# First stage of a two-block network on one core: x loaded in rows and turned on the chip, its splits in written order, angles behind them, the recurrence's constants in a feed forward

## The chip, the cores and the metric

The kernel runs on one core of a Trainium2 chip. The metric is the device time of one execution in microseconds (us), as the median of several runs. Of the engines, TensorE (PE) multiplies and transposes, VectorE (DVE) and ScalarE (ACT) work elementwise, GpSimd (POOL) does a few small operations, and SyncE (SP) issues the transfers.

## The reference, cut to what matters

x has 256 tokens of width 1024. The whole network is two blocks of four sublayers; the first block begins with the even mixer, and the change lies there and in one corner of the sublayer behind it and of the odd mixer.

```python
def even_mixer(xn, positions, w_in, w_out, ...):          # xn = rms_norm(x, norm_mix_pre[0])
    z = (xn @ w_in)                                       # 1024 -> 2048: q, k, v, u of 512 each
    q, k = partial_rope(q, positions) * HEAD_DIM**-0.5, partial_rope(k, positions)
    att = dilated_attention(q, k, v)
    ssm = s5_mixer(u, a_re, a_im, log_dt, ...)            # a_bar = exp(A * dt): sin and cos of angles
    return concatenate([att, ssm]) @ w_out

def rglru_mixer(...):                                     # in the odd mixer, after the first feed forward
    log_a = -RG_C * gate_r * softplus(-lam)               # softplus(-lam): constants of 1024 channels
    ...
x = x + rms_norm(mix, norm_mix_post)                      # then swiglu, the odd mixer, swiglu, and block two
```

## The kernel before, in words

The 256 tokens are two halves of 128 rows. A product in float32 is made of three in a faster format: each operand is split into a high half and a low half, and TensorE adds high times high, high times low and low times high. The weights stand in one array in the order in which they are used, and SP loads them (`raw_weights`, L277) into four buffers `wr` of 128x1024. ScalarE copies the high half `wh`, VectorE subtracts and writes the low half `wl` (`weights`), and six buffers hold such halves; a `wr` buffer is free when its `wl` is made. Names such as `wl_538` carry the number of a tile; `pm` are sums in PSUM, `pt` transposes in PSUM, `s`, `b`, `c` and `j` buffers in SBUF, `cpk` the packed constants.

A list scheduler orders each engine by priorities and by its own estimate of when operands are ready; the transfers on SP stay in program order unless something lets them move. Each engine then works in that order and waits wherever an operand is missing.

The stage begins in `even_mixer`. `first_linear` (L1123) makes u, the last 512 columns, from `xT`, an input that holds x already turned (channels in rows): for k = 0 and 1 a product in full float32, for k = 2 to 7 the split one. Two transposes of u on VectorE (L1172), the angles (`pos` L1162, `sincos` L575) and the setup of the recurrence's matrices of s5 (`s5_setup`) follow. The projections to k (512 to 1024), q (0 to 512) and v (1024 to 1536) take x's rows for the squares (loaded at L1165; ScalarE squares `x` into `j`) and the turned and split x for the products; k and q are turned by an angle (rope: four products and two sums of 128x64 on VectorE per half) and transposed by TensorE (L227). Then come the attention over memory, the dilated attention and the s5 states.

Some work is issued through lists with due times (`later`, `need`): s5's pieces, and `memory_whole`, which loads `memT` (L813), scales it by 16 operations of ScalarE and splits it. The small constants of the odd mixer's recurrence are written in `odd_mixer` (L1302), but depend on `cpk` alone.

Of the kernel before, what the change touches and what calls it, by code (L numbers as in the profile page):

```python
# [17 lines left out]
P = 128  # L18
# [123 lines left out]
class Net:  # L142
# [222 lines left out]
    def spread_rows(self, r):  # L365

        out, d = self.slot(), self.slot()
        for h in HALVES:
            self.ts(d[:, h * P : (h + 1) * P], self.ident, r[h], ALU.mult)
# [205 lines left out]
    def sincos(self, ang, sin, cos, tmp):  # L575
# [5 lines left out]
        self.act(sin, ang, AF.Sin)  # L581
        self.stt(tmp, ang, -1.0, ang, ALU.mult, ALU.max)
        self.ts(tmp, tmp, -1.0, ALU.mult, 0.5 * math.pi, ALU.add)
        self.act(cos, tmp, AF.Sin)
# [218 lines left out]
    def remember(self):  # L803

        self.mem_x = self.first_operand("memT", "mem_norm", TUNE["mem"])
# [24 lines left out]
    def s5_exps(self):  # L830
# [13 lines left out]
        self.act(self.lru_e, self.lru_e, AF.Exp, scale=-1.0)  # L844

    def s5_setup(self):
# [152 lines left out]
        nc.gpsimd.memset(self.TO, 0.0)  # L999
# [123 lines left out]
    def first_linear(self, gain, mat, c0, c1, whole):  # L1123
# [3 lines left out]
        k = 0  # L1127
        while k < KD:
            n = 1 if k < whole else min(2, KD - k)
            t = self.slot()  # L1130
            self.nc.sync.dma_start(out=t[:, : n * 256], in_=self.ins["xT"][:, k * 256 : (k + n) * 256])
            for i in range(n):
                (hi, lo), a = X.both(k), t[:, i * 256 : (i + 1) * 256]
                if k < whole:
                    ((raw, _, _),) = self.raw_weights([(mat, k * P, c0, c1)])
                    b = t[:, 256:512]
                    self.ts(b, a, g[k], ALU.mult)
                    for h in HALVES:
                        self.mmul(ps[h], b[:, h * P : (h + 1) * P], raw[:, : c1 - c0], k == 0, False)
                    self.act(hi, b)  # L1140
                    self.sub(lo, b, hi.bitcast(F32))
                else:
                    (ws,) = self.weights([(mat, k * P, c0, c1)])
                    self.act(hi, a, scale=g[k])
                    self.stt(lo, a, g[k], hi.bitcast(F32), ALU.mult, ALU.subtract)
                    for h in HALVES:
                        self.mm3(ps[h], X.span(h, k), ws, False, k == KD - 1)
                k += 1
        return X, ps

    def even_mixer(self):
# [8 lines left out]
        X, ps = self.first_linear("mix_pre0", "ev_w_in", 1536, 2048, 2)  # L1160
        pos_i = pool.tile([P, 2], I32, name="pos_i")
        nc.sync.dma_start(out=pos_i, in_=self.ins["pos"])  # L1162
        ahead = self.weights([("ev_w_in", k * P, 512, 1024) for k in range(4)])
        for i in HALVES:
            nc.sync.dma_start(out=self.x[i], in_=self.ins["x"][i])  # L1165
        for i in HALVES:
            R.append(self.rsqrt(self.sumsq([self.x[i][:, 0:512], self.x[i][:, 512:1024]], D), 1))
        for h in HALVES:
            u = self.slot()
            self.act(u, ps[h], scale=R[h])  # L1170
            for g in (0, 1):
                nc.vector.transpose(  # L1172
                    U2[g].rearrange("p (b j) -> p b j", b=8)[:, :, h * 32 : h * 32 + 32], u[:, g * 256 : (g + 1) * 256]
                )


        pos = pool.tile([P, 2], F32, name="pos")
        nc.vector.tensor_copy(pos, pos_i)
        ang, sin, cos, tmp = (pool.tile([P, 32], F32, name=n) for n in ("ang", "sin", "cos", "sctmp"))
        nc.vector.tensor_copy(ang[:, 16:32], self.s5_base[0])  # L1180
        for h in HALVES:
            self.ts(ang[:, h * 8 : h * 8 + 8], self.col("inv_freq", 0, 8), pos[:, h : h + 1], ALU.mult)
        self.sincos(ang, sin, cos, tmp)
        self.rsin, self.rcos = sin[:, 0:16], cos[:, 0:16]
        self.s5_turn = sin[:, 16:32], cos[:, 16:32], tmp[:, 16:32]
        self.s5_bc = self.big()
        nc.sync.dma_start(out=self.s5_bc[:, 0:1024], in_=self.ins["s5_bc"])
# [30 lines left out]
        nc.sync.dma_start(out=bias, in_=self.ins["dil_bias"])  # L1218
# [4 lines left out]
        turns, inner = self.s5_setup()  # L1223
# [78 lines left out]
    def odd_mixer(self, X, R):  # L1302
        nc = self.nc

        lam = self.col("lam", 0, 8)
        e = self.lru_e
        m4, m4h, hbr, hbi, s, s2 = (
            self.const.tile([P, 8], F32, name=n) for n in ("m4", "m4h", "hbr", "hbi", "lru_s", "lru_s2")
        )
        self.ts(s, e, 2.0, ALU.add)  # L1310
        nc.vector.reciprocal(s, s)
        self.mul(s, s, e)
        self.mul(s2, s, s)
        self.ts(e, s2, 1.0 / 19.0, ALU.mult, 1.0 / 17.0, ALU.add)
        for n in (15, 13, 11, 9, 7, 5, 3, 1):
            self.mul(e, e, s2)
            self.ts(e, e, 1.0 / n, ALU.add)
        self.mul(e, e, s)
        self.ts(s, lam, 0.0, ALU.min)
# [518 lines left out]
```

## Time and profile before

| | |
|---|---|
| median of 3 runs | 1256.41 us (1255.8 to 1257.54) |
| profiled execution | 1257.49 us, of which its span is 1255.70 |
| busy: TensorE, VectorE, ScalarE | 1238.2, 879.7, 766.5 us |
| TensorE, 0 to 65 us | busy 58.76 us |
| transferred | 216.83 MB, mean 173 GB/s |

The span is the time from the first instruction of the profiled execution to its last; the profiled execution's own time holds 1.79 us more. TensorE is busy nearly all of it, so the table is read for the few stretches in which it is not, most of which lie in the first 60 us.

### The profile page before, as it was taken

How to read it: one execution, taken by the hardware profiler on the slowest of the kernel's cores; microseconds unless marked ns; L12 is line 12 of the kernel's file. 1: busy time of each engine (PE TensorE's matmuls, PEld its weight loads, DVE VectorE, ACT ScalarE, POOL GpSimd, SP SyncE). 2: the span in 40 equal slices, each digit the busy share in tenths (PEclk: the TensorE clock that was granted, in tenths of full speed). 3: DMA queues.
4: the chain of work that ended last, by engine and by line, in shares of the span. 5: the costliest groups of instructions: out<-in, count | busy, mean ns of one | idle time of the engine just before them, and what ended most of it. 6: DMA issues, size and time to landing. Idle time of an engine off the chain costs nothing.

```text
span 1255.7 us, 17972 instructions
## 1 busy us (share of the span) xinstructions
PE 1238.2 (99%) x6526; PEld 1036.8 (83%) x6526; DVE 879.7 (70%) x1579; ACT 766.5 (61%) x1446; POOL 52.3 (4%) x64
## 2 busy tenths in 40 slices
PE   8999999999999999999999999999999999999998
PEld 6776888888889788888887788888888888888887
DVE  7897578775588977776477855777746865677752
ACT  6767577554488766555378845555536675655541
POOL 1000000000000100000013100000000100000000
PEclk9999999999999999999999999999999999999999
DMA  8614357666555556666545224656664532666562
GB/s 272 228 54 149 119 200 235 192 193 207 160 184 173 166 187 219 190 193 203 183 151 177 85 68 151 211 191 188 210 191 152 182 118 81 201 199 191 186 196 71
DMA packets 63065, 216.83 MB, mean 173 GB/s; under 512 B 7136, under 2 KB 7520, under 8 KB 62976
## 3 DMA queue, kind: packets, MB, share of 16 engines
q1 hardware_dynamic: 62976, 215.68, 54.2%
q8 instruction: 51, 0.84, 0.3%
q14 instruction: 38, 0.31, 0.1%
HBM read 214.61 MB, written 1.05 MB: 172 GB/s over the span
## 4 chain that ended last, share of the span: by engine, by line
PE 86%; DVE 5%; ACT 4%; DMA 3%; issue 1%; POOL 1%; SPq 0%; ACTq 0%; DVEq 0%; POOLq 0%
PE pm L220 82%; PE pt L227 3%; DVE wl L195 2%; ACT b L217 1%; ACT j L217 1%; DVE s L195 1%; ACT wh L217 1%; ACT s L217 1%; DMA wr<-in_wall_dram 1%; DVE b L212 1%; POOL m L414 1%; DMA s<-in_memT_dram 0%; DMA x<-in_x_dram 0%; DMA s<-in_xT_dram 0%; DMA s<-in_rope_dram 0%
## 5 line engine op out<-in xcount | busy, mean ns | idle before, releaser
L195 DVE TENSOR_TENSOR wl<-wr,wh 128x1024 fp32r<-128x1024 f32 (+2 forms) x389 | 467.2, 1206 | 208.9 <-ACT wh L217 208.1
L220 PE MATMUL pm<-wh,b 128*128 128x512 f32 (+2 forms) x1788 | 574.1, 395 | 3.7 <-ACT wh L217 2.1
L217 ACT ACTIVATE wh<-wr 128x1024 fp32r<-128x1024 f32 (+2 forms) x381 | 397.4, 1047 | 263.7 <-PE pm L220 139.4
L220 PE MATMUL pm<-b,wh 128*128 128x512 f32 (+1 forms) x1440 | 453.2, 372 | 0.0
L220 PEld LDWEIGHTS pm<-wh,b 128*128 128x128 f32 x1788 | 333.7, 188 | 72.6 <-ACT wh L217 4.5
L220 PE MATMUL pm<-b,wl 128*128 128x256 f32 x1296 | 359.6, 278 | 0.0
L220 PE MATMUL pm<-wl,b 128*128 128x512 f32 (+2 forms) x894 | 348.2, 390 | 2.5 <-DVE wl L195 2.5
L220 PEld LDWEIGHTS pm<-b,wh 128*128 128x128 f32 x1440 | 261.1, 188 | 50.7 <-ACT b L217 0.3
L220 PEld LDWEIGHTS pm<-b,wl 128*128 128x128 f32 x1296 | 243.8, 188 | 0.3
L220 PEld LDWEIGHTS pm<-wl,b 128*128 128x128 f32 x894 | 168.2, 188 | 36.6 <-DVE wl L195 5.0
L195 DVE TENSOR_TENSOR s<-pm,s 128x256 f32<-128x256 f32 (+1 forms) x164 | 74.0, 453 | 35.5 <-ACT s L217 19.8
L217 ACT ACTIVATE s<-pm 128x256 f32<-128x256 f32 (+1 forms) x152 | 58.6, 387 | 65.0 <-PE pm L220 64.8
L414 POOL TENSOR_TENSOR m<-m,mhalf 128x1 f32<-128x1 f32 (+3 forms) x54 | 48.2, 892 | 979.6 <-DVE m L209 767.4
L195 DVE TENSOR_TENSOR s<-s,s 128x512 f32<-128x512 f32 (+3 forms) x90 | 60.5, 672 | 2.5
L217 ACT ACTIVATE b<-pt,cpk 128x128 fp32r<-128x128 f32 (+2 forms) x138 | 48.3, 391 | 9.2 <-DVE b L212 5.4
L217 ACT ACTIVATE j<-pm,m 128x128 f32<-128x128 f32 (+1 forms) x94 | 36.8, 406 | 22.3 <-PE pm L220 19.6
L227 PE MATMUL pt<-ident,s 128*128 128x128 f32 x288 | 44.8, 280 | 3.2 <-DVE s L195 1.7
L212 DVE SCALAR_TENSOR_TENSOR b<-pt,cpk,b 128x128 fp32r<-128x128 f32 x122 | 37.9, 344 | 11.7 <-ACT b L217 11.2
L227 PEld LDWEIGHTS pt<-ident,s 128*128 128x128 f32 x288 | 34.7, 144 | 13.7 <-issue 3.1
L217 ACT ACTIVATE j<-x 128x512 f32<-128x512 f32 x32 | 20.2, 631 | 27.2 <-DVE x L212 14.1
L220 PE MATMUL pm<-s,b 128*128 128x256 f32 (+1 forms) x160 | 34.6, 337 | 0.0
L220 PE MATMUL pm<-wr,s 128*128 128x512 f32 x72 | 34.1, 610 | 0.2 <-DMA wr<-in_wall_dram 0.2
(162 smaller groups left out, 810.7 us busy)
## 6 DMA issues: line engine op xcount, KB each, us to landing
wr<-in_wall_dram SPq DMA_DIRECT2D x381, 512.0 KB, 4.1
wr<-in_wall_dram SPq DMA_DIRECT2D x11, 256.0 KB, 3.4
s<-in_memT_dram SPq DMA_DIRECT2D x8, 256.0 KB, 6.1
s<-in_gpost_dram SPq DMA_DIRECT2D x8, 256.0 KB, 5.4
wr<-in_wall_dram SPq DMA_DIRECT2D x4, 384.0 KB, 2.9
x<-in_x_dram SPq DMA_DIRECT2D x2, 512.0 KB, 6.6
s<-in_mem_dram SPq DMA_DIRECT2D x4, 256.0 KB, 5.8
out_dram<-x SPq DMA_DIRECT2D x4, 256.0 KB, 2.0
```

Source lines behind the costliest of these rows:

```text
L195: return self.nc.vector.tensor_tensor(out=out, in0=a, in1=b, op=op)
L212: return self.nc.vector.scalar_tensor_tensor(out=out, in0=a, scalar=s, in1=b, op0=op0, op1=op1)
L217: return self.nc.scalar.activation(out, a, func, **kw)
L220: self.nc.tensor.matmul(out, lhsT, rhs, start=start, stop=stop)
L227: self.nc.tensor.transpose(out, a, self.ident)
L414: self.nc.gpsimd.tensor_tensor(out=z, in0=w, in1=self.mhalf[:, 0:n], op=ALU.pow)
```

## The change

x comes in rows only: the loads of `xT` and the later two of x go, and `first_linear` loads pieces of x's rows (`load`) and turns them on TensorE (`turn`, four transposes into one PSUM tile). The readers of the turned x read PSUM. The weights of u for k = 4 to 7 come as two loads of 128x1024. The whole of `first_linear`, the weights of k, the squares and the transposes of u are in written order on VectorE, TensorE and ScalarE. The angles and `s5_setup` are issued only behind that, and the constants of the recurrence behind a mark in the first feed forward (`lru_setup`, from `remember`).

```diff
     def remember(self):
+        with self.tc.issue_after(self.mark.ins):
+            self.lru_setup()
         self.mem_x = self.first_operand("memT", "mem_norm", TUNE["mem"])
...
-    def first_linear(self, gain, mat, c0, c1, whole):
+    def first_linear(self, gain, mat, c0, c1, whole, between):
...
-            t = self.slot()
-            self.nc.sync.dma_start(out=t[:, : n * 256], in_=self.ins["xT"][:, k * 256 : (k + n) * 256])
...
+        def load(k, n):
+            for h in HALVES:
+                cols = slice(k * P, (k + n) * P)
+                self.nc.sync.dma_start(out=self.x[h][:, cols], in_=self.ins["x"][h, :, cols])
+        def turn(k):
+            pt = self.transpose4([self.x[h][:, i * P : (i + 1) * P] for i in (k, k + 1) for h in HALVES])
+            return [pt[:, 0:256], pt[:, 256:512]]
+        load(0, 2)
+        pt = turn(0)
...
+            coming = {0: (2, 2), 2: (4, 4)}.get(k)
...
+                    ks = [k] if k < 4 else [k, k + 1]
+                    ws = dict(zip(ks, self.weights([(mat, i * P, c0, c1) for i in ks])))
+                if coming:
+                    load(*coming)
+                self.act(hi, a, scale=g[k])
+                self.stt(lo, a, g[k], hi.bitcast(F32), ALU.mult, ALU.subtract)
...
+            if more:
+                ahead = turn(k + 2)
+            elif k % 2:
+                pt = ahead
+            between(k)
...
-        for i in HALVES:
-            nc.sync.dma_start(out=self.x[i], in_=self.ins["x"][i])
...
+        with self.tc.manual_schedule(engines={nc.vector.engine, nc.tensor.engine, nc.scalar.engine}):
+            X, ps = self.first_linear("mix_pre0", "ev_w_in", 1536, 2048, 2, between)
...
+        with self.tc.issue_after(turned.ins), self.tc.issue_after(evicted.ins):
+            angles()
...
-        turns, inner = self.s5_setup()
+        with self.tc.issue_after(turned.ins), self.tc.issue_after(evicted.ins):
+            turns, inner = self.s5_setup()
...
-        for _ in range(9):
+        for _ in range(8):
             self.mmul(idle[:, 0:P], self.ones, self.ones, True, True)
```

TensorE at the start of the program, before the change (`s` holds the scaled x of k = 0 and 1, `b` the halves of the later ones):

```order
L220 MATMUL pt_95<-ones 128x128 x9
L220 MATMUL pm_125<-wr_130,s_127 128x512
L220 MATMUL pm_126<-wr_130,s_127 128x512
L220 MATMUL pm_125<-wr_139,s_137 128x512
L220 MATMUL pm_126<-wr_139,s_137 128x512
L220 MATMUL pm_125<-wh_150,b_129 128x512
L220 MATMUL pm_126<-wh_150,b_129 128x512
L220 MATMUL pm_125<-wl_151,b_129 128x512
```

The same place after the change (`x_108` and `x_109` are the rows of the two halves):

```order
L220 MATMUL pt_95<-ones 128x128 x8
L227 MATMUL pt_136<-ident,x_108 128x128
L227 MATMUL pt_136<-ident,x_109 128x128
L227 MATMUL pt_136<-ident,x_108 128x128
L227 MATMUL pt_136<-ident,x_109 128x128
L220 MATMUL pm_132<-wr_142,s_146 128x512
L220 MATMUL pm_133<-wr_142,s_146 128x512
L227 MATMUL pt_152<-ident,x_108 128x128
L227 MATMUL pt_152<-ident,x_109 128x128
L227 MATMUL pt_152<-ident,x_108 128x128
L227 MATMUL pt_152<-ident,x_109 128x128
L220 MATMUL pm_132<-wr_157,s_159 128x512
```

The transposes of the second pair of k stand between the products of k = 0 and those of k = 1.

VectorE, the end of the angles and the rope, before the change; `lru` tiles belong to the recurrence, `wl_244` to the weights of k, `ang` and `sctmp` to the angles:

```order
L208 TENSOR_SCALAR lru_e<-lru_e 128x8
L212 SCALAR_TENSOR_TENSOR ang<-sctmp,ang 128x32
L195 TENSOR_TENSOR lru_e<-lru_e,lru_s_3416 128x8
L209 TENSOR_SCALAR ang<-ang 128x32
L208 TENSOR_SCALAR lru_e<-lru_e 128x8
L212 SCALAR_TENSOR_TENSOR sctmp<-ang 128x32
L195 TENSOR_TENSOR lru_e<-lru_e,lru_s_3416 128x8
L209 TENSOR_SCALAR sctmp<-sctmp 128x32
L208 TENSOR_SCALAR lru_e<-lru_e 128x8
L195 TENSOR_TENSOR wl_244<-wr_239,wh_243 128x1024
```

The same after it; `wl_538` is the first of the weights of v, `s_374` the half of k that is turned first, `c` are constants of s5:

```order
L948 COPY b_123<-c_114 128x512
L212 SCALAR_TENSOR_TENSOR ang<-sctmp,ang 128x32
L948 COPY b_123<-c_114 128x512
L209 TENSOR_SCALAR ang<-ang 128x32
L195 TENSOR_TENSOR wl_538<-wr_529,wh_537 128x1024
L212 SCALAR_TENSOR_TENSOR sctmp<-ang 128x32
L949 MEMSET b_123 128x8 x2
L209 TENSOR_SCALAR sctmp<-sctmp 128x32
L195 TENSOR_TENSOR s_376<-s_374,sin 128x64
L195 TENSOR_TENSOR s_376<-s_374,cos 128x64 x2
L195 TENSOR_TENSOR s_376<-s_374,sin 128x64
L195 TENSOR_TENSOR c_611<-c_113,cos 128x16
```

The angles have moved from ahead of the weights of k to behind those of q, and the rope follows them directly.

ScalarE around the scalings of memT (`s_499` to `s_512` before, `s_505` to `s_518` now), before the change:

```order
L217 ACTIVATE b_302<-pt_477 128x512
L217 ACTIVATE s_489<-pm_458,m_271 128x512
L217 ACTIVATE b_300<-b_662,cpk 128x16x16 x2
L217 ACTIVATE s_499<-s_499,cpk 128x128 x4
L217 ACTIVATE s_500<-s_500,cpk 128x128 x4
L217 ACTIVATE s_511<-s_511,cpk 128x128 x4
L217 ACTIVATE s_512<-s_512,cpk 128x128 x4
L217 ACTIVATE b_302<-pt_566 128x512
L217 ACTIVATE s_303<-pm_547,m_261 128x512
L217 ACTIVATE b_720<-b_662,cpk 128x4x16x16 x2
```

And after it:

```order
L217 ACTIVATE b_308<-pt_483 128x512
L217 ACTIVATE s_495<-pm_464,m_281 128x512
L217 ACTIVATE s_505<-s_505,cpk 128x128 x4
L217 ACTIVATE s_506<-s_506,cpk 128x128 x4
L217 ACTIVATE s_517<-s_517,cpk 128x128 x4
L217 ACTIVATE s_518<-s_518,cpk 128x128 x4
L217 ACTIVATE b_308<-pt_572 128x512
L217 ACTIVATE s_309<-pm_553,m_265 128x512
L217 ACTIVATE b_283<-b_668,cpk 128x16x16 x2
L217 ACTIVATE b_726<-b_668,cpk 128x4x16x16 x2
```

The two copies of 128x16x16 into `b` (`b_300` before, `b_283` now) have moved from ahead of the 16 scalings to behind them.

## Rows read from the trace of the kernel before

**Rows 1.** The page: engines, then the chain by engine.

```profile
PE 1238.2 (99%) x6526; PEld 1036.8 (83%) x6526; DVE 879.7 (70%) x1579; ACT 766.5 (61%) x1446; POOL 52.3 (4%) x64
...
PE 86%; DVE 5%; ACT 4%; DMA 3%; issue 1%; POOL 1%; SPq 0%; ACTq 0%; DVEq 0%; POOLq 0%
```

**Rows 2.** Windows of all engines: window, length, busy us (instructions); PEclk, DMA share, GB/s.

```profile
25.00:30.00 5.00, 3.17 (x14) 1.98 (x13) 4.86 (x14) 4.94 (x9) 2.31 (x2) 1.00 0.84 304
...
55.00:60.00 5.00, 3.58 (x15) 2.31 (x13) 1.89 (x11) 5.00 (x11) 0.00 (x0) 1.00 0.10 35
...
165.00:200.00 35.00, 34.91 (x180) 28.92 (x179) 26.69 (x46) 24.57 (x44) 0.55 (x1) 1.00 0.64 213
10.00:45.00 35.00, 31.83 (x140) 24.65 (x141) 33.51 (x134) 27.53 (x47) 2.90 (x3) 1.00 0.85 291
```

**Rows 3.** Waits of TensorE, 0 to 62 us: total, times, longest.

```profile
PE pm L220 <- ACT wh L217: 2.1, 2, 1.1
...
PE pm L220 <- DVE wl L195: 1.1, 2, 0.7
```

**Rows 4.** The chain in order of time: start, us, what.

```profile
3.07 5.95 DMA s<-in_xT_dram
...
15.64 6.22 DMA x<-in_x_dram
...
28.04 9.37 PE pm L220 x40
...
45.68 6.26 DMA s<-in_memT_dram
51.96 4.80 ACT s L217 x16
57.81 2.09 ACT b L217 x2
```

**Rows 5.** Timeline of TensorE: start, us, line, operation, count [idle before].

```profile
7.60 1.96 PE L220 MATMUL pm<-wr,s 128*128 128x512 f32 x4 [0.15 <-DMA wr<-in_wall_dram]
...
18.89 0.84 PE L220 MATMUL pm<-wh,b 128*128 128x512 f32 x3
...
37.24 0.60 PE L227 MATMUL pt<-ident,s 128*128 128x128 f32 x4
...
59.95 1.09 PE L227 MATMUL pt<-ident,b 128*128 128x128 f32 x8 [1.43 <-ACT b L217]
```

**Rows 6.** Groups of VectorE by form, 0 to 22 us: busy us, mean ns.

```profile
L195 DVE TENSOR_TENSOR wl<-wr,wh 128x1024 fp32r<-128x1024 f32 x2 | 2.4, 1222 | 0.4 <-ACT wh L217 0.4
...
L195 DVE TENSOR_TENSOR lru_e<-lru_e,lru_s 128x8 f32<-128x8 f32 x9 | 1.5, 161 | 0.1
...
L195 DVE TENSOR_TENSOR b<-s,b 128x256 fp32r<-128x256 f32 x2 | 0.8, 421 | 0.0
L923 DVE COPY b<-c 128x512 f32<-128x512 f32 x2 | 0.8, 418 | 0.0
L208 DVE TENSOR_SCALAR s<-s,cpk 128x256 f32<-128x256 f32 x2 | 0.7, 354 | 1.2 <-DMA s<-in_xT_dram 1.2
```

**Rows 7.** Groups of ScalarE by form, 0 to 62 us: busy us, mean ns.

```profile
L217 ACT ACTIVATE wh<-wr 128x1024 fp32r<-128x1024 f32 x12 | 12.5, 1054 | 3.1 <-DVE sctmp L208 2.0 <-DMA wr<-in_wall_dram 0.6 <-PE pm L220 0.4
...
L217 ACT ACT_TABLE_LOAD x2 | 2.6, 1283 | 0.7 <-PEq L1710 0.7
```

**Rows 8.** Timeline of VectorE and ScalarE.

```profile
22.52 0.21 ACT L217 ACTIVATE cos<-sctmp 128x32 f32<-128x32 f32 x1
...
34.14 0.22 DVE L195 TENSOR_TENSOR s<-s,cos 128x64 f32<-128x64 f32 x1
...
46.91 0.90 ACT L217 ACTIVATE b<-b,cpk 128x256 f32<-128x256 f32 x2
```

**Rows 9.** DMA: those issued on SP at 2.59 and 7.85 us: KB, us to landing.

```profile
wr<-in_wall_dram SPq DMA_DIRECT2D x1, 256.0 KB, 4.9
...
s<-in_xT_dram SPq DMA_DIRECT2D x1, 256.0 KB, 4.4
```

More of the change, by code (lines that the diff above doesn't have):

```diff
@@ L572, in project_out, with reduce_angle @@
         return self.rows_out(Y, mat, range(Y.K) if order is None else order, tail, gp, gains)
-    def sincos(self, ang, sin, cos, tmp):
+    def reduce_angle(self, ang, tmp):
         self.ts(tmp, ang, 1.0 / (2.0 * math.pi), ALU.mult, ROUND, ALU.add)
@@ L998, in s5_setup @@
         self.TO = self.big()
-        nc.gpsimd.memset(self.TO, 0.0)
+        for i in range(4):
+            nc.gpsimd.memset(self.TO[:, i * 512 : (i + 1) * 512], 0.0)
         t4 = self.TO.rearrange("p (b r c) -> p b r c", b=16, r=4)
@@ L1181, in even_mixer, with angles @@
-        for h in HALVES:
-            self.ts(ang[:, h * 8 : h * 8 + 8], self.col("inv_freq", 0, 8), pos[:, h : h + 1], ALU.mult)
-        self.sincos(ang, sin, cos, tmp)
         self.rsin, self.rcos = sin[:, 0:16], cos[:, 0:16]
         self.s5_turn = sin[:, 16:32], cos[:, 16:32], tmp[:, 16:32]
-        self.s5_bc = self.big()
-        nc.sync.dma_start(out=self.s5_bc[:, 0:1024], in_=self.ins["s5_bc"])
+        def angles():
+            nc.vector.tensor_copy(pos, pos_i)
+            nc.vector.tensor_copy(ang[:, 16:32], self.s5_base[0])
+            for h in HALVES:
+                self.ts(ang[:, h * 8 : h * 8 + 8], self.col("inv_freq", 0, 8), pos[:, h : h + 1], ALU.mult)
+            self.reduce_angle(ang, tmp)
+            self.act(sin, ang, AF.Sin)
+            self.act(cos, tmp, AF.Sin)
@@ new lines, in between @@
+        def between(k):
+            if k == 3:
+                nc.sync.dma_start(out=pos_i, in_=self.ins["pos"])
+        with self.tc.manual_schedule(engines={nc.vector.engine, nc.tensor.engine, nc.scalar.engine}):
+            X, ps = self.first_linear("mix_pre0", "ev_w_in", 1536, 2048, 2, between)
+            ahead = []
+            for i in HALVES:
+                ahead += self.weights([("ev_w_in", k * P, 512, 1024) for k in (2 * i, 2 * i + 1)])
+                R.append(self.rsqrt(self.sumsq([self.x[i][:, 0:512], self.x[i][:, 512:1024]], D), 1))
+            self.s5_bc = self.big()
+            self.tc.keep_in_program_order(nc.sync.dma_start(out=self.s5_bc[:, 0:1024], in_=self.ins["s5_bc"]))
+            for h in HALVES:
+                u = self.slot()
+                evicted = self.act(u, ps[h], scale=R[h])
+                for g in (0, 1):
+                    turned = nc.vector.transpose(
+                        U2[g].rearrange("p (b j) -> p b j", b=8)[:, :, h * 32 : h * 32 + 32], u[:, g * 256 : (g + 1) * 256]
+                    )
@@ L1217, in even_mixer @@
         self.linear(X, "ev_w_in", 0, 512, q_sink)
[L1218 removed]
+        self.tc.keep_in_program_order(nc.sync.dma_start(out=bias, in_=self.ins["dil_bias"]))
         whole = self.memory_whole()
@@ L1303, in odd_mixer @@
         nc = self.nc
[L1305 to L1319, printed above, removed]
-        self.ts(s, s, 4.0, ALU.mult)
-        self.stt(m4, e, -8.0, s, ALU.mult, ALU.add)
-        self.ts(m4h, m4, -0.5, ALU.mult)
-        self.ts(hbr, self.col("b_r", 0, 8), 0.5, ALU.mult)
-        self.ts(hbi, self.col("b_i", 0, 8), 0.5, ALU.mult)
+        m4, m4h, hbr, hbi = self.lru_cols
         v8 = lambda t: t.rearrange("p (k t) -> p k t", k=8)
```

80 lines of the change are left out of this document (41 added, 39 removed).

## The prediction

> **What bounds the kernel now.** I read the page first: TensorE is busy 99% of the span and the chain that ended last runs 86% through it [rows 1], so a microsecond is won or lost only where TensorE waits or gets more to do. Then the windows of the first 65 us, where the change lies: the two with most idle time are 25 to 30 us (1.83 us missing) and 55 to 60 us (1.42 missing), with the granted clock at 1.00, the upper of its two levels, 2.4 GHz, in both [rows 2]. Then the waits of TensorE up to 62 us: 2.1 us for halves `wh` that ScalarE makes, 1.1 for `wl` of VectorE [rows 3], and 1.43 for a `b` of ScalarE [rows 5]. Last the chain in order of time [rows 4]. Its early part shows two transfers as bounds: xT until 9.0 us, and the load of x (15.64 to 21.86), behind which the squares and the weights' halves are late. From 45.68 on it shows another: memT is loaded (6.26 us), ScalarE scales it in 16 operations (4.80), makes two wide copies `b` (2.09), and TensorE, done with v, has waited for these 1.43 us when it goes on at 59.95 [rows 4, 5]. After that it is dense to the end of the stage. So the change is worth what it does to two times: when TensorE ends k, q and v, and when ScalarE ends those two copies.
>
> **The first product.** Before, xT came turned. Now TensorE turns x, and the order shows where: four transposes stand ahead of the products of k=0, four ahead of those of k=1. TensorE works in order, so the products of k=1 queue behind the second four, which want x's columns 256 to 512. These are the fifth and sixth transfers, and up to their end the queue has carried 0.89 MB (cpk 0.10, x 4 x 0.13, weights 0.26). Before, the same 0.89 MB had landed when the second weights did, 2.59 + 4.9 = 7.5 us [rows 9]. The weights of k=1 are next, 1.15 MB; that much had landed at 3.07 + 5.95 = 9.0 [rows 4]. So k=1 runs from about 9.1 us, against 7.60 [rows 5]: +1.5 us. The sixteen transposes themselves are 16 x 0.15 = 2.4 us (four took 0.60 [rows 5]); those behind k=2 and k=4 fall into time in which TensorE waits anyhow, so I add only what the sum below has.
>
> One read may be dearer: VectorE's two scalings of 128x256 now read PSUM; from SBUF they took 0.354 us [rows 6]. The Trainium skill, "VectorE: DVE Perf Modes", section "Why PSUM operands drop a tier", says that a PSUM operand takes float32 down to the slowest mode. The subtraction of the same shape costs 0.421 [rows 6]; by that the two cost 0.13 more, lost in the range.
>
> From k=4 on two weights of 128x512 come as one 128x1024. The first is the thirteenth transfer; 2.7 MB are through by about 12.9 us (an estimate: before, 2.46 MB had landed at 12.25, 7.85 + 4.4 [rows 9], and another 0.26 MB take 0.7). In written order ScalarE makes `wh` (1.05 [rows 7]), then the high halves of x; VectorE makes `wl` (1.22 [rows 6]), then the low halves (about 0.48 each), and each waits for the other in turn. Laid end to end: `wh` 13.95, `wl` 15.2, low halves 15.7 and, after ScalarE's second high half at 16.2, 16.7; the next pair `wh` 17.2, `wl` 18.45, low halves 18.95 and 19.95; the last six products (6 x 0.23) end at 21.2. Before, u's last product started at 18.89 and k's first followed it at 19.1 [rows 5]. So **+2.1 us**.
>
> **What k gets back.** Behind u the weights wait ready, and the load of x that held k up is gone. Dense, a product takes 0.23 (40 in 9.37 [rows 4]), so k's 48 take 10.9 and end near 32.1. Before, k took 14.0, from 19.1 to 33.1 (22 of the 40 dense ones from 28.04 on are k's), because of waits of 1.1 for `wh` and 1.1 in two for `wl` [rows 3] and the 0.9 that the restarts cost. All of it goes: **-3.1**, and a lead of 1.0 is left.
>
> **The angles.** Before, VectorE made them between 16 and 19 us, and cos was ready at 22.7 [rows 8], 14 us before k was turned. Now they stand behind u's transposes, between the weights' `wl`, and one row of it decides: `wl` 538 (weights of v) stands ahead of the last two angle operations, and on ScalarE its `wh` stands ahead of the table load. By my hand schedule ScalarE is dense from 19.5 on: eight `wh` of 1.05 [rows 7] with four squares, three evictions and scalings of s5_bc between them. It ends `wh` 537 at 36.3, then a scaling of 0.5 and the table load, 1.28 [rows 7]: sin near 38.2. VectorE ends the fourth q `wl` at 35.05, eight small operations (0.16), a 0.28 and two copies (0.418) [rows 6] bring it to 37.1, `wl` 538 to 38.2, the last two to 38.65; cos at 38.95. Four rope products and two sums take 1.2 more (0.22 each, started 0.135 apart [rows 8]): 40.15. TensorE has by then 23 of q's products behind it, at 37.3, and the transposes of the turned k stand next. It waits **2.9 us**, where it waited for nothing (37.24 [rows 5]). With the four transposes it is at 40.8; before, it had the same products and eight transposes done at 39.3, so, less the second four, the lag is 2.0.
>
> **memT, and the sum.** The memT issue waited on SP for a weight buffer that the fourth v `wl` frees, at 45.3; it was issued at 45.68 [rows 4]. In the new order the rope of two tiles, some 20 constants of s5 (0.16 each) and four `wl` of 1.22 lie between cos and that `wl`: it ends near 47.2 to 48.2. So memT is 1.9 to 2.9 late. Behind its 16 scalings there now also stand two copies, 0.90 in all, that ScalarE made at 46.91 before, while it idled [rows 8]: 0.9 more, as the order of ScalarE shows. The 1.43 of wait before 59.95 [rows 5] is no slack here: it is this chain that it waits for. So TensorE goes on from there between 1.9 + 0.9 = 2.8 and 2.9 + 0.9 = 3.8 later; **I take +3.2**, nearer the lower end, since some of VectorE's constants overlap in pairs. v's own products, 2.0 late, end within that.
>
> **What costs nothing, and why.** The 28 constants of the recurrence (about 4.5 us of VectorE at 0.16 [rows 6]) go to the first feed forward: from 165 to 200 us VectorE is busy 26.69 of 35 us and TensorE 34.91 [rows 2], so they lie in VectorE's gaps; without that cover they would cost 4.5, and I allow 0 to 1. The transfers are 1.05 MB less, 3 us of transfer, but behind 13 us no wait in the sum ends with a transfer. One idle product less is 0.47 us early, while TensorE waits for data. From TensorE's 120th microsecond on the orders are the same, and TensorE is full, so the lag stays to the end. The profiled execution took 1257.49 (span 1255.70 and 1.79 around it), 1.08 over the median of 1256.41; 1257.49 + 3.2 = 1260.7 for one like it, and **1259.6** against the median.
>
> **Rivals.** 0.2% is 2.5 us, about what a measurement of this kernel tells from no change.
> *A, the forecast, 0.46:* the two waits as above, +2.5 to +4.5: 1258.9 to 1260.9.
> *B, half of it, 0.26:* the early transfers land about 1 us sooner (the queue no longer alternates two kinds of tile), or VectorE's small operations overlap as before; TensorE waits 1 to 2 us for the turned k and memT is 1 late: 0 to +2.5, 1256.4 to 1258.9, the same.
> *C, faster, 0.16:* VectorE, not the chain of angles, is what the stage hangs on: from 10 to 45 us it is busy 33.51 of 35 us [rows 2]. Sixteen of the recurrence's operations, 2.6 us by 0.161 [rows 6], stood in just that stretch. If VectorE is as full without them and fills its own 1.49 us of gaps, memT comes 4 us sooner, less the 0.9: -3.1, about 1253.3. It decides where VectorE idles less than 3 us from 10 to 45 us; by my schedule it idles some 5, waiting between `wh` and `wl` from 13 to 20 us. That is the weakest part of my sum.
> *D, a lead that stays small, 0.05:* cos is ready in time and memT unchanged: -0.5 to -2, the same.
> *E, the clock, 0.07:* TensorE now waits twice for about 3 us, where its longest wait so far was 1.43 and the granted clock stayed at 1.00 [rows 2, 5]. A stretch at the lower level, 1.2 GHz, doubles each product of 0.234 [rows 4]; twenty of them cost 4.7, so +5 to +8: 1261.4 to 1264.4. The Trainium skill, "TensorE: Matmul & The Clock Gate", section "HAM oscillation — how this bites in real kernels", tells of a kernel whose waits between bursts of products bring the lower clock back each time; no row here shows it.
>
> Chances: slower A and E, 0.53; same B and D, 0.31; faster C, 0.16. The range 1253.4 to 1262.6 leaves out about half of C and most of E.
>
> **What would show it.** Right: the first transposes near 4.8 us and k=1's products at 9 or later; u's end near 21; a TensorE wait of 2 to 3.5 us before the transposes of turned k near 40, released by VectorE's rope; cos near 39; memT issued at 47 to 49; the wait before the eight transposes of `b` near 62.5 to 63.5. Wrong: a TensorE that reaches those eight transposes before 60.5; VectorE full between 13 and 20 us; a granted clock under 1.00 in any window. A difference that arises after 65 us, for instance a TensorE wait in the first feed forward, would prove wrong that the rest is untouched.

## The result, and the profile after

The changed kernel takes 1262.81 us (median of 5 runs, 1261.01 to 1265.74), the kernel before 1256.41: the ratio is 1.0051, with a 95% interval of 1.0040 to 1.0061. It is 6.4 us slower, outside the predicted range. The profiled execution took 1262.81 us with a span of 1261.0, against 1255.7 before.

First the place where most of the wait was forecast. The timeline of TensorE after the change (start, length, operation, count, and in brackets the idle time before it with its releaser); the rows answer to [rows 5]:

```profile
4.63 0.76 PE L227 MATMUL pt<-ident,x 128*128 128x128 f32 x4
5.96 1.98 PE L220 MATMUL pm<-wr,s 128*128 128x512 f32 x4 [0.58 <-DVE s L208]
...
8.22 1.88 PE L220 MATMUL pm<-wr,s 128*128 128x512 f32 x4
...
38.16 0.63 PE L227 MATMUL pt<-ident,s 128*128 128x128 f32 x4 [1.82 <-DVE c L195]
...
58.92 1.09 PE L227 MATMUL pt<-ident,b 128*128 128x128 f32 x8 [1.25 <-ACT b L217]
...
93.78 1.13 PE L220 MATMUL pm<-b 64*128 64x256 f32 x4 [0.76 <-ACT b L217]
96.09 3.32 PE L220 MATMUL pm<-b 64*128 64x256 f32 x12 [1.19 <-DVE s L195]
99.35 5.10 PE L220 MATMUL pm<-wr,s 128*128 128x512 f32 x6
```

The new wait before the transposes of the turned k is there, 1.82 us. But TensorE is at the eight transposes of `b` at 58.92, where it was at 59.95: in this execution the changed kernel is 1.03 us ahead when the forecast had it 2.8 to 3.8 behind. The loss comes 35 us later, at two waits of 0.76 and 1.19 us in the s5 states and the dilated attention. The windows of all engines show what they bring; first after, then before (window, length, busy us and count of PE, PEld, DVE, ACT, POOL, then granted clock, DMA share, GB/s):

```profile
36.00:38.00 2.00, 0.34 (x2) 0.00 (x0) 1.83 (x14) 1.52 (x5) 0.00 (x0) 1.00 0.68 207
38.00:40.00 2.00, 1.84 (x10) 1.63 (x11) 2.00 (x11) 2.00 (x5) 0.00 (x0) 1.00 0.65 233
...
91.00:97.00 6.00, 4.05 (x27) 3.01 (x27) 6.00 (x15) 4.58 (x16) 1.02 (x1) 1.00 0.27 90
97.00:104.00 7.00, 7.00 (x16) 3.49 (x13) 3.93 (x13) 5.29 (x22) 1.01 (x1) 0.51 0.00 0
104.00:128.00 24.00, 23.89 (x137) 16.97 (x137) 13.96 (x36) 16.79 (x36) 0.00 (x0) 1.00 0.54 176
```

```profile
91.00:97.00 6.00, 5.88 (x37) 3.73 (x35) 5.80 (x16) 3.89 (x20) 1.01 (x1) 1.00 0.28 87
97.00:104.00 7.00, 6.96 (x16) 3.14 (x17) 3.54 (x13) 4.41 (x17) 1.01 (x1) 1.00 0.26 76
```

TensorE misses 1.95 us from 91 to 97 where it missed 0.12, and for the 7 us behind that the granted clock is 0.51, the lower level of 1.2 GHz, where it was 1.00. At half speed 7 us do the work of 3.6, so some 3.4 us are lost to the clock and about 1.8 to the waits, 5.2 in all; the lead of 1 us pays for a part, and 4.2 of the 5.3 us between the two spans are accounted for. The full-width products that follow start at 99.35 (above); before, at 97.04:

```profile
97.04 9.28 PE L220 MATMUL pm<-wr,s 128*128 128x512 f32 x21
```

The longer of those waits is for VectorE; the shorter ends with a copy `b` that ScalarE makes, behind one of VectorE's small sums. VectorE's timeline where the first state of s5 is summed and scanned, after and then before (`pm<-pm,s` of 32x128 is the first of four small sums of the skip term into `pm`, SCAN the recurrence):

```profile
77.91 0.29 DVE L195 TENSOR_TENSOR pm<-pm,s 32x128 f32<-32x128 f32 x1 [2.13 <-PE pm L220]
78.12 0.67 DVE L195 TENSOR_TENSOR s<-s,s 128x512 f32<-128x512 f32 x1
78.82 0.69 DVE L195 TENSOR_TENSOR s<-pm,b 128x512 f32<-128x512 f32 x1
79.43 1.21 DVE L1064 TENSOR_TENSOR_SCAN s<-b,s 128x512 f32<-128x512 f32 x1
...
95.37 0.67 DVE L195 TENSOR_TENSOR s<-pm,dil_bias 128x512 f32<-128x512 f32 x1
```

```profile
76.17 0.68 DVE L195 TENSOR_TENSOR s<-s,s 128x512 f32<-128x512 f32 x1
76.88 0.69 DVE L195 TENSOR_TENSOR s<-pm,b 128x512 f32<-128x512 f32 x1
77.49 1.21 DVE L1038 TENSOR_TENSOR_SCAN s<-b,s 128x512 f32<-128x512 f32 x1
78.94 0.29 DVE L195 TENSOR_TENSOR pm<-pm,s 32x128 f32<-32x128 f32 x1 [0.23 <-PE pm L220]
...
93.85 0.69 DVE L195 TENSOR_TENSOR s<-pm,dil_bias 128x512 f32<-128x512 f32 x1 [0.17 <-PE pm L220]
```

Before, the state sum and the first scan stand ahead of the small sum, which waits for late products of TensorE; after, they stand behind it. So VectorE idles 2.13 us with the sum's operands ready, the scan starts at 79.43 in place of 77.49 although TensorE is ahead, VectorE is full from there on, and the first sum of the dilated scores with `dil_bias` is made at 95.37 in place of 93.85. The last two small sums are late as well, at 90.77 and 94.51 in place of 87.17 and 89.68. No line of the diff reorders these operations: the order is the scheduler's, and which of its estimates the change moved was not looked at. Word for word from the orders of VectorE, after and before (`s_916` and `s_907` are the state that is summed, `b_123` and `b_124` carry the decay, and the scan is listed as a SCALAR_TENSOR_TENSOR of L1064 and L1038):

```
L195 TENSOR_TENSOR pm_876<-pm_876,s_775 32x4x32
L195 TENSOR_TENSOR s_916<-s_916,s_918 128x512
L195 TENSOR_TENSOR s_918<-pm_898,b_673 128x512
L1064 SCALAR_TENSOR_TENSOR s_925<-b_123,s_916 128x512
```

```
L195 TENSOR_TENSOR s_907<-s_907,s_909 128x512
L195 TENSOR_TENSOR s_909<-pm_889,b_667 128x512
L1038 SCALAR_TENSOR_TENSOR s_916<-b_124,s_907 128x512
L195 TENSOR_TENSOR pm_867<-pm_867,s_769 32x4x32
```

### The profile page after: what moved, and what is told of

It reads as the page before. It is cut to its first block, busy times and chain, and to the rows that moved or that the text cites. A ratio compares the mean times of both kernels' runs of the same rounds, so it can differ in the third digit from the quotient of the medians.

```text
span 1261.0 us, 17991 instructions
## 1 busy us (share of the span) xinstructions
PE 1242.2 (99%) x6540; PEld 1040.6 (83%) x6540; DVE 878.9 (70%) x1577; ACT 765.1 (61%) x1444; POOL 52.5 (4%) x67
## 4 chain that ended last, share of the span: by engine, by line
PE 85%; DVE 6%; ACT 4%; DMA 2%; issue 1%; POOL 1%; SPq 0%; ACTq 0%; POOLq 0%; DVEq 0%
PE pm L220 81%; PE pt L227 4%; DVE wl L195 2%; DVE s L195 2%; ACT wh L217 2%; DMA wr<-in_wall_dram 1%; ACT b L217 1%; ACT j L217 1%; ACT s L217 1%; DVE b L212 1%; POOL m L414 1%; PE pt L220 0%; DMA s<-in_rope_dram 0%; DMA s<-in_memT_dram 0%; DVE b L1465 0%
## 5 line engine op out<-in xcount | busy, mean ns | idle before, releaser
L217 ACT ACTIVATE b<-pt,cpk 128x128 fp32r<-128x128 f32 (+3 forms) x144 | 51.1, 395 | 12.0 <-DVE b L212 8.5
L212 DVE SCALAR_TENSOR_TENSOR b<-pt,cpk,b 128x128 fp32r<-128x128 f32 (+1 forms) x128 | 40.8, 351 | 12.3 <-ACT b L217 11.9
L217 ACT ACTIVATE j<-x 128x512 f32<-128x512 f32 x32 | 20.2, 630 | 26.9 <-DVE x L212 14.3
```

What stands on the lines that cost most here:

```text
L212: return self.nc.vector.scalar_tensor_tensor(out=out, in0=a, scalar=s, in1=b, op0=op0, op1=op1)
L217: return self.nc.scalar.activation(out, a, func, **kw)
```

## The experiments

My theory after the result: the order of VectorE in the s5 states, with the clock that falls behind its waits, makes most of the loss, and the first stage a smaller part. The rival: the late angles are the cause, and the late waits only follow from them. Ratios are to the kernel before in the same batch, with 95% intervals; 0.001 is 1.26 us.

**e1, the order of the states put back.** The changed kernel with the pieces of s5 that hold the small sums due later, which puts sum and scan ahead again.

```diff
-    "s5c": 4.0,
+    "s5c": 4.6,
```

> The changed kernel with one number of its due times altered (the inner products of s5 fall due just behind the first group of states instead of just ahead), so that VectorE finds the sums of the states and the first scan ahead of the small sum in pm that waited 2.13 us for TensorE at 75.8 us. Theory A (the loss comes from VectorE's order in the s5 states, which makes the dilated scores' sums late, TensorE runs dry at 93 to 96 us and its clock falls): the 2.13 us of VectorE go, the first sum with dil_bias starts near 93.3 instead of 95.4, TensorE waits under 0.5 us between 91 and 97, the granted clock stays at 1.00, and the time is 5 to 7 us under the changed kernel, about 1256 to 1257 or a little under the kernel before. Theory B (the clock falls for something earlier, the waits at 38 and 58 us or the transposes): the clock falls all the same and the time stays within 2 us of the changed kernel's 1262.8.

Measured: 1259.88 us (11 runs, 1256.01 to 1261.23), ratio 1.0016 (1.0007 to 1.0025). The late loss is gone, as Theory A had it: from 97 to 104 us TensorE is busy 6.66 of 7 us at full clock. But the time is some 3 us above its 1256 to 1257. In this execution it was the wait of the first stage that brought the lower clock. Windows, then the timeline of TensorE:

```profile
40.00:42.00 2.00, 2.00 (x7) 1.79 (x8) 2.00 (x10) 1.77 (x5) 0.00 (x0) 0.53 0.59 223
42.00:44.00 2.00, 2.00 (x7) 1.50 (x6) 1.56 (x14) 0.35 (x2) 0.00 (x0) 0.62 0.82 227
...
97.00:104.00 7.00, 6.66 (x20) 3.26 (x19) 5.25 (x14) 4.43 (x17) 1.94 (x2) 1.00 0.01 2
```

```profile
39.99 1.00 PE L227 MATMUL pt<-ident,s 128*128 128x128 f32 x4 [2.44 <-DVE c L195]
61.93 1.10 PE L227 MATMUL pt<-ident,b 128*128 128x128 f32 x8 [0.83 <-ACT b L217]
```

The wait is 2.44 here against 1.82 above, and the eight transposes come at 61.93, near the forecast of 62.5 to 63.5. So two executions with one order of the first stage stand 3 us apart there, and whether the wait of the first stage brings the clock down differs from one to the next. The 11 runs spread with the mean granted clock: 1256.01 at 0.999, 1261.23 at 0.997.

**e2, idle products in the late wait.** The changed kernel with four products of 128x128 on a constant behind the last scores of the first group (`last`), while TensorE would wait.

```diff
+        filler = self.tbank()
+        with self.tc.issue_after(last.ins):
+            for _ in range(FILL):
+                self.nc.tensor.matmul(filler[:, 0:P], self.ones, self.ones, start=True, stop=True)
```

> The changed kernel with four idle products of 128x128 (about 1.9 us) put on TensorE between the two groups of dilated scores, where it waited 0.76 and 1.19 us; nothing reads them. VectorE's order and its lateness are unchanged. Theory A (waits first, and then the clock that they bring down): the granted clock stays at 1.00 from 97 to 104 us, the 3.4 us that 6.85 us at the lower level cost come back, and the time is about 1259.5. Theory B (the waits themselves are the loss, and the clock only a small part, or it falls for another reason): the time stays within 1 us of 1262.8, or rises by the filler.

Measured: 1260.93 us (6 runs, 1258.96 to 1267.77), ratio 1.0043 (1.0023 to 1.0063). Window, then the timeline of TensorE:

```profile
97.00:104.00 7.00, 6.07 (x28) 4.04 (x28) 6.11 (x15) 5.57 (x18) 2.03 (x2) 1.00 0.13 53
```

```profile
6.26 3.78 PE L221 MATMUL pm<-wr,s 128*128 128x512 f32 x4 [0.58 <-DVE s L209]
...
99.88 2.38 PE L221 MATMUL pm<-b 64*128 64x256 f32 x12 [0.93 <-DVE s L196]
```

The clock stays at 1.00 from 97 to 104 us although a wait of 0.93 is left, so in this execution the fall there was kept away. The interval covers the changed kernel's 1.0051, and the profiled execution again had a longer wait at the turned k (2.39, then 0.50 of clock from 42 to 44 us) and the eight transposes at 62.70. Its four products of k=0 also took 3.78 us where those of the changed kernel's profile took 1.98 (above). What the late clock alone is worth is not told apart by it.

**e3, the recurrence's constants back.** The changed kernel with `lru_setup` called from the odd mixer again.

```diff
-        with self.tc.issue_after(self.mark.ins):
-            self.lru_setup()
...
+        self.lru_setup()
```

> The changed kernel with the 28 small operations of the recurrence written in the odd mixer again, as before; the scheduler then puts 26 of them on VectorE ahead of the first scaling of the turned x. If their move is what keeps the first stage on time: 26 chained operations of about 0.2 us run from 3.2 to 8.4 us, the products of k=0 start near 8.9 instead of 5.96, and u, k and q end some 2 to 3 us later; the time is 1 to 4 us above the changed kernel's 1262.8 unless VectorE makes it up before 91 us. If the place of these operations doesn't matter, the first stage ends within 0.5 us of the changed kernel's and so does the time.

Measured: 1266.66 us (4 runs, 1264.65 to 1267.97), ratio 1.0077 (1.0063 to 1.0091). By the ratios that is 3.3 us above the changed kernel, within the 1 to 4 of the first of the two cases. The scheduler puts the small operations ahead of VectorE's first scaling of x, 26 of them in one chain; TensorE waits 3.33 us for it at k=0, and 2.88 before the transposes of turned k, with the clock at 0.50 behind both:

```profile
9.01 3.05 PE L220 MATMUL pm<-wr,s 128*128 128x512 f32 x4 [3.33 <-DVE s L208]
...
43.13 0.63 PE L227 MATMUL pt<-ident,s 128*128 128x128 f32 x4 [2.88 <-DVE c L195]
```

In the written order of the new first stage the constants have to go; that part of the change repairs a cost that the order itself would bring.

**e4, the late order alone, on the kernel before.** The first state sum is issued behind the first small sum (`added`), which is where the change had put it; the product `xi` of the same state is written ahead of it, as it stood there too.

```diff
-            self.add(xr, xr, t)
             self.mul(v(xi), v(S[1]), E)
+            if g == 0:
+                with self.tc.issue_after(self.added.ins):
+                    self.add(xr, xr, t)
+            else:
+                self.add(xr, xr, t)
```

> The kernel before with one thing of the changed kernel's order: VectorE's first sum of the s5 states and with it the first scan are queued behind the small sum in pm of the inner products. Nothing else is changed. Theory A (this order and not the first stage makes the loss): VectorE waits some 2 us more near 77 us, the first sum with dil_bias comes at 95 or later instead of 93.85, TensorE waits 1 to 2 us there, and if the clock falls with it the time is 4 to 6 us above the kernel before, 1260 to 1262; if it doesn't fall, 1 to 2 us above. Theory B (the first stage's loss is carried): no difference beyond 1 us.

Measured: 1261.57 us (5 runs, 1259.96 to 1262.74), ratio 1.0034 (1.0022 to 1.0047). One addition of 0.67 us in another place, with the scans that then come behind it, costs 4.3 us. Windows and timeline of TensorE:

```profile
91.00:97.00 6.00, 5.06 (x30) 3.51 (x30) 6.00 (x15) 3.59 (x17) 1.01 (x1) 0.92 0.26 87
97.00:104.00 7.00, 7.00 (x13) 3.29 (x13) 3.96 (x13) 4.93 (x21) 1.01 (x1) 0.58 0.00 0
```

```profile
95.53 3.32 PE L220 MATMUL pm<-b 64*128 64x256 f32 x8 [0.94 <-DVE s L195]
```

A like wait and a like fall of the clock as in the changed kernel, with the first stage as it was. With e1 (1.0051 less 1.0016 is 0.0035) the two sides agree: 4.3 to 4.4 of the 6.4 us are this order, and 2.0 are the first stage. The intervals leave 2.8 to 5.9 for the order by e4, and 0.9 to 3.1 for the first stage by e1.

**e5 and e6, the transposes of turned k and q put off.** Both have them some 20 products later, so that TensorE works on q while the angles are made; e6 has the edit of e1 besides.

```diff
-    "qk": 3.8,
+    "qk": 9.0,
```

> The changed kernel with the transposes of the turned k and q put off by 19 products of TensorE (their due time 9.0 in place of 3.8), so that the late angles are waited for behind other work; the order of VectorE in the s5 states is as in the changed kernel. My theory (the s5 order makes the loss, the angles a smaller part): the wait before the transposes of turned k, 1.82 us in the changed kernel, falls below 0.5 us, the granted clock stays at 1.00 from 36 to 46 us, the waits of about 0.8 and 1.2 us near 94 to 96 us and the granted clock of 0.50 behind them stay: 1260 to 1262 us, ratio to the kernel before 1.003 to 1.005. Rival (the angle wait is the cause and the late waits follow from it): the late waits go too, 1255 to 1257 us, ratio 0.999 to 1.001.

> The changed kernel with both edits: the transposes of turned k and q put off, and the pieces of s5 that hold the small inner sums due 0.6 later (4.6 in place of 4.0), so that the first state sum and scan stand ahead of them on VectorE. My theory: neither of the two losses is left, clock 1.00 in every window up to 130 us; the eight transposes of b come at 57 to 59 us (59.95 before, less the wait that is gone, bounded by the copies behind the arrival of memT), and the lead is kept: 1253.5 to 1256 us, ratio 0.9975 to 0.9995. Rival (memT's chain or a third wait takes it back): eight transposes at 60 us or later, ratio 1.000 to 1.002.

Measured: e5 1264.37 us (5 runs, 1263.01 to 1265.42), ratio 1.0056 (1.0044 to 1.0069); e6 1259.54 (11 runs, 1258.0 to 1263.55), ratio 1.0021 (1.0011 to 1.0031). The wait for the angles is gone in both, and neither is faster for it. In e5 the late waits of 0.8 and 1.2 us stay, as the theory had it and not the rival; but its first stage is no better either, and the time is above the theory's 1262. The timelines of TensorE, e5 and then e6:

```profile
59.88 1.97 PE L227 MATMUL pt<-ident,b 128*128 128x128 f32 x8 [3.93 <-ACT b L217]
```

```profile
61.79 1.97 PE L227 MATMUL pt<-ident,b 128*128 128x128 f32 x8 [4.21 <-ACT b L217]
```

TensorE comes early and waits 4 us for the copies of `b`, and the eight transposes behind that take 1.97 us in place of 1.09: the clock has fallen here (0.51 from 60 to 66 us in e5, 0.72 in e6). My 1253.5 to 1256 us for e6 fell; its rival, memT's chain, is what the rows show. A part of e6's lateness is older: its four products of k=0 took 3.78 us, as e2's did.

**e9 and e11, memT's loads ahead of the memory product's weights.** e9 is e6 with the four loads (L813, the last of them `memory_load`) first on SP, e11 the changed kernel with that alone.

```diff
-        self.mem_kv = [self.memory_kv(0, False, whole, between)]
+        with self.tc.issue_after(self.memory_load.ins):
+            self.mem_kv = [self.memory_kv(0, False, whole, between)]
```

> The changed kernel with the transposes put off and the small inner sums later, as in the run before (1259.5, eight transposes of b at 61.79 after a wait of 4.2 us), and with the four loads of memT ahead of the four weights of the memory product on SP instead of behind them. My theory (the wait is memT's: its scalings stand ahead of the copies of b on ScalarE, and its issue at 46.9 is late): memT is issued at 37 to 40 us, its 16 scalings end before 52, the wait of 4.2 us falls below 1.5 us, eight transposes at 56.5 to 58.5, clock 1.00 from 28 to 104 us: 1253.5 to 1256 us, ratio 0.997 to 0.9995. Rival (the copies wait for the powers of s5 on VectorE, which follow from the late angles): wait 3 us or more stays, eight transposes at 60.5 or later, 1258 to 1260 us, ratio 1.001 to 1.0025.

> The changed kernel with memT's loads ahead of the four weights of the memory product and nothing else. My theory: the angle wait (1.8 to 2.4 us before the transposes of turned k) stays and decides when TensorE comes to the eight transposes, 57 to 61 us, with a wait under 0.7 us there; the small inner sum still stands ahead of the first scan on VectorE, so the waits of 0.8 and 1.2 us near 95 us and the granted clock of 0.50 behind them stay: 1260.5 to 1263 us, ratio 1.003 to 1.005. Rival (memT was the root of the loss): 1256 to 1258 us.

Measured: e9 1257.29 us (11 runs, 1254.52 to 1261.49), ratio 1.0002 (0.9991 to 1.0013); e11 1262.46 (6 runs, 1259.42 to 1266.54), ratio 1.0050 (1.0032 to 1.0068). In e9 memT is issued at 34.73, ScalarE has scaled it by 49.3, and the wait is 1.46. The chain of e9 in order of time shows what then ends last:

```profile
49.14 0.51 DVE c L195 x6
49.82 0.60 DVE b L195
...
54.41 0.88 DVE b L195
55.31 2.68 ACT b L217 x3
58.04 1.09 PE pt L227 x8
```

These are the powers of s5's angles on VectorE, so the rival of e9 (the copies follow from the late angles) has a part in what is left. The wait and the eight transposes, 58.04, are where the theory had them; the time lies between its 1256 and the rival's 1258. e11 has no wait at the eight transposes, keeps late ones (0.76 and 0.48 us, and a clock of 0.63 from 97 to 104), and gains nothing that can be measured: memT is not the root of the loss. In its profile VectorE waits only 0.33 us for the small sum and is as late behind it: its first product of the states comes at 75.39, in the changed kernel's profile at 73.89. So an idle time of 2.13 us need not stand ahead of the late waits; work put off to there, perhaps by the late angles, does as much. With the order put right, as in e9, they are gone but for 0.15 us, although the angles are late.

**e7, e8, e10 and e12, the controls on the kernel before.** e7 moves the recurrence's constants into the feed forward, e8 puts the transposes of turned k and q off, e10 puts memT's loads first, e12 is e7 and e10 together; their edits are the ones quoted above.

> The kernel before with one part of the change alone: the recurrence's constants moved into the first feed forward, so that VectorE has some 25 small operations fewer in the first 30 us. VectorE's order in the s5 states stays as before (sum and scan ahead of the small inner sum). My theory: the time moves by less than 1 us, 1255.5 to 1257 us, ratio 0.9992 to 1.0005, and the feed forward hides the operations. Rival (VectorE's small operations hold TensorE in the first stage, as the prediction's rival of a faster kernel had it): the waits of k at 25 to 31 us go and TensorE reaches the eight transposes 1 to 3 us earlier, 1253.5 to 1255.5 us.

> The kernel before with the transposes of turned k and q put off (due time 9.0 in place of 3.8) and nothing else: the control for the two kernels of the change that have this edit. My theory: before has its angles at 22 us, so nothing is gained there; within 1 us of before, ratio 0.9992 to 1.0008, if the order of the s5 states on VectorE stays as it is (it does in the list). Rival (later transposes are better in themselves, whatever the angles): 1253.5 to 1255.5 us.

> The kernel before with the loads of memT ahead of the four weights of the memory product, the control for the run above. My theory: the wait of 0.6 us before its eight transposes goes, nothing else: 1255.5 to 1256.8 us, ratio 0.999 to 1.0. Rival (the order of SP is worth more in itself, through the waits of 48 to 62 us): 1253 to 1255 us, ratio 0.997 to 0.999.

> The kernel before with two edits that were run alone: memT's loads ahead of the four weights of the memory product (alone 1255.0 us, ratio 0.9981), and the recurrence's constants in the feed forward (alone 1256.5, ratio 0.9994). My theory (VectorE's small operations never held TensorE: the waits of k on wh and wl stay, 2.6 and 1.4 us with the constants moved against 2.1 and 1.1 before): no more than with memT alone, 1254.5 to 1256 us, ratio 0.9975 to 0.9985, and the waits of k at 25 to 31 us stay at 2 us or more in sum. Rival (the relief of VectorE was there, but hidden behind memT): waits of k under 1.5 us, 1252 to 1254 us, ratio 0.9955 to 0.997.

| kernel | us, median | runs | ratio | interval |
|---|---|---|---|---|
| e7, constants moved | 1256.53 | 11 | 0.9994 | 0.9982 to 1.0006 |
| e8, transposes put off | 1257.49 | 11 | 1.0000 | 0.9991 to 1.0009 |
| e10, memT's loads first | 1255.04 | 11 | 0.9981 | 0.9973 to 0.9990 |
| e12, e7 and e10 | 1255.14 | 12 | 0.9985 | 0.9976 to 0.9994 |

e7: taking some 25 operations from VectorE's first stage moves nothing beyond the interval, and the waits of TensorE for `wh` and `wl` stay, as the theory said (2.6 and 1.4 us up to 62 us, 1.42 of them in u, ahead of k). e8: putting the transposes off is worth nothing in itself. Its order of the s5 states did change: the first scan stands behind the first small sum, for which VectorE idles 1.36 us, while the later small sums keep their order. From 91 to 97 us TensorE is still busy 5.85 of 6 us, so one scan behind one small sum is not enough for the loss. e10 is faster than the kernel before by 0.19%: my theory had at most 0.1%, and the rival was right that the order on SP is worth more in itself. TensorE is at the eight transposes at 57.56 without a wait, against 59.95 in [rows 5]:

```profile
57.56 1.04 PE L227 MATMUL pt<-ident,b 128*128 128x128 f32 x8
```

Not all of its 2.4 us is this wait: eight of e10's 11 runs have a mean clock of 1.000, with a median of 1254.70, and six of the 23 of the kernel before, with 1255.72, so among runs of full clock 1.0 us is left; the rest comes with fewer runs of lower clock, and why they are fewer isn't shown.

e12 brings no more than e10: with memT out of the way the relief of VectorE is worth nothing that can be measured. Its profile has no wait of k at 25 to 31 us, where I had expected 2 or more; its one wait for weights is u's, 1.69 us at 10.5, and behind it the clock is 0.50, so that TensorE begins k at 20.7 in place of 19.1 and may only have come too late to wait. That is the rival's sign without the rival's time.

## Why the prediction was wrong, point by point

**The step that failed** is the last of the sum, "so the lag stays to the end": it carries the lag of the eight transposes near 60 us on with no term for what lies between them and TensorE's 120th microsecond, and I had compared no order there. TensorE's products there are nearly the same, but VectorE's order from 76 us on is not: small sums stand ahead of the first state sum and the scans, TensorE waits 0.76 and 1.19 us near 95, and the clock falls to 0.51. That costs 4.3 us (e4), more than the 3.2 of the whole sum. From there on the step holds: with the two profiles matched product by product, TensorE is 4.6 us late where the kernel before is at 105 us, and 5.2 where it is at 1250. The terms of the first stage were off the other way, 2.0 us by e1 for the 3.2; 4.3 and 2.0 make up the 6.4 but for 0.1. Three of the prediction's own signs of being wrong came: the transposes before 60.5, a clock under 1.00, and a difference that arises after 65 us.

**The first product:** early. First transposes at 4.63 (4.8 forecast), k=1's products at 8.22 and not 9.1. TensorE comes to the transposes of turned k at 38.16 - 1.82 = 36.34 in place of 37.3; since k's 48 and q's 23 products ahead of them are dense, u ended near 20.2 and not 21.2: this term was +1.1, not +2.1. In e1, with the same order, k begins 1.2 us later (at 21.3 in place of 20.1, by count of the products), and there +2.1 was right. The scaling that reads PSUM takes 0.48 us where the subtraction of my bound took 0.421 and the scaling from SBUF 0.354 [rows 6]; two of them cost 0.25 more than before where that bound gave 0.13. The rule cited from the Trainium skill, "VectorE: DVE Perf Modes", section "Why PSUM operands drop a tier", agrees in kind, and the cost is lost in the range, as I said.

**What k gets back:** right. No wait of TensorE from 14 to 36 us is left.

**The angles:** the wait is there, released by VectorE's rope and constants, but 1.82 us long in the profiled execution, where cos starts at 36.82 and not 38.95; in e1, e2 and e3 it is 2.44, 2.39 and 2.88 against 2.9.

**memT:** in the profiled execution issued at 45.35 and not at 47.2 to 48.2, and landed in 4.63 us where I took 6.26 [rows 4]; the two copies do stand behind the scalings. In e1 and e2, with the same first stage, memT is issued at 48.77 and 49.44 and TensorE goes on at 61.93 and 62.70, 2.0 and 2.75 later than before, against my 2.8 to 3.8. And e1, which lacks the late loss, is 0.0016, or 2.0 us, slower than before. The chains in order of time tell the two executions apart, the changed kernel's first and then e1's:

```profile
7.98 3.69 DMA wr<-in_wall_dram
...
38.79 1.85 PE pm L220 x8
...
45.35 4.63 DMA s<-in_memT_dram
```

```profile
8.28 4.60 DMA wr<-in_wall_dram
...
40.99 3.07 PE pm L220 x8
...
48.77 4.35 DMA s<-in_memT_dram
```

Of the 3.4 us by which memT is issued later in e1, 1.8 arise ahead of the transposes of turned k, 1.2 of them with the weights that land later at 12.9 us; 1.6 arise behind these transposes, at the lower clock. For memT's issue waits for a `wl`, that for a `wh`, and ScalarE makes this `wh` behind a copy of what TensorE has transposed. So the chain of this part is the one that I named, but that e1 and e2 come within 1.2 us of my 3.2 is in part luck: their size holds a cost of the clock that the sum had left out.

**The rivals.** B (half of it, 0 to +2.5) is what the first stage alone comes to, by e1. C (VectorE hangs the stage) fails by its own condition: from 10 to 45 us VectorE is busy 28.25 of 35 us in the changed kernel and idles 6.75, where C wanted less than 3; e7 and e12 gain nothing from its relief either. E (the clock falls) happens, and I gave it 0.07: at the place that I named in e1, e2 and e3, and at one that I had not thought of in the changed kernel's profile. That the measured 1262.81 lies in E's 1261.4 to 1264.4 is luck, since its sum had no late wait. I priced it at 4.7 us for twenty products; the windows of the changed kernel show some 3.4. The rule cited there from the Trainium skill, "TensorE: Matmul & The Clock Gate", section "HAM oscillation — how this bites in real kernels", agrees in kind with these rows, 0.53 behind e1's wait of 2.44 us and 0.51 behind the waits at 93 to 96 us.

**What is open.** e9 has every repair that I found, and stands where the kernel before stands; but e10, with memT's loads alone on the kernel before, is 0.0021, some 2.6 us, ahead of it. The chain of e9 and its runs (1254.52 at a mean clock of 1.000, 1261.49 at 0.995) point to the late angles, their powers and the clock: three of e9's 11 runs have a mean clock of 1.000, with a median of 1255.02, near e10's 1254.70. But the angles were not put back early by themselves, so this cause isn't shown. Nor is it shown why the products of k=0 run slowly in some executions (below).

## What to carry to other kernels

Where a list scheduler orders the engines, compare the order of every engine to the end of the dependent work, not only where the diff stands: an edit in one place let it exchange others some 40 us later, and a small operation ahead of the first one of a chain can cost more than the whole sum of the edit's own terms. Price a new wait of TensorE with the stretch of lower clock behind it, not by its length alone. And look for what ends last behind a wait before removing it: the covered angles only uncovered memT's chain, whose four loads, placed first, gained 2.4 us on the old kernel without any of the change.

## What the runs showed of the hardware

The granted clock fell behind waits of TensorE that were short. It fell to 0.50 to 0.53 behind 3.93, 2.88, 2.44 and 2.39 us (e5, e3, e1, e2), and stayed at 1.00 behind 1.82 (after), 1.58 (e11) and 1.46 (e9), and 1.43 before [rows 2, 5]. But early in u it also fell to 0.50 behind 1.76 and 1.69 us (e8, e12). The rows of e8, timeline and window:

```profile
10.55 0.73 PE L220 MATMUL pm<-wh,b 128*128 128x512 f32 x2 [1.76 <-ACT wh L217]
```

```profile
12.00:14.00 2.00, 2.00 (x7) 1.54 (x6) 2.00 (x6) 1.82 (x5) 0.00 (x0) 0.50 0.82 196
```

Between the narrow products of the dilated scores shorter waits went ahead of a fall: 0.94 us in e4, 0.76 and 1.19 in the changed kernel; in e2, where idle products stood in the same gap, a wait of 0.93 left it at 1.00. The length of one wait alone does not tell it.

The start differs from execution to execution too. In e2, e6 and e11 the four products of k=0, the first behind the idle ones, take 3.71 to 3.78 us; in the profiles of the changed kernel, e1, e5 and e9 they take 1.98. Nearly twice the time is what the lower clock level would give; but the windows show 1.00 there, so no row of the clock shows it. In the six profiles with the first stage of the kernel before, at most 1 us is lost that way (e4, eight products in 4.69 us; e7, in 3.67). With one idle product less and transposes behind them this may be a cost of the change; no run tested it.

The spread of single executions is larger than I had reckoned: e4 has the first stage of the kernel before unchanged, and is at the eight transposes at 58.94 where that one was at 59.95. A good part of it goes with the clock. The 23 runs of the kernel before that were measured beside e9 have a median of 1255.72 us at a mean clock of 1.000 (6 runs), 1257.23 at 0.999 (11) and 1258.72 at 0.997 (4). And its profile has a stretch of lower clock itself, far from the change:

```profile
694.00:701.00 7.00, 5.66 (x24) 4.65 (x25) 4.21 (x10) 4.51 (x19) 1.97 (x2) 0.76 0.35 112
```
